# When the first layer's output weight is split: six of eight slices during the last gates instead of four

## The chip, the cores and the metric

The kernel runs on one core of a Trainium2 chip. Five engines work side by side, each through its own list of instructions in order: TensorE (PE in the profile; PEld is its weight load), VectorE (DVE), ScalarE (ACT), GpSimd (POOL) and SyncE (SP), which here mostly issues DMAs. The metric is the device time of one execution in microseconds, the median of several.

## The reference, cut to what matters

One inference step of two layers, a Mamba-2 SSD layer and a latent-attention (MLA) layer, over 1024 prompt tokens and 64 sample tokens (8 sequences of 8). The change touches the end of the SSD layer alone:

```
proj = einsum('btd,de->bte', h, w_in)          # z, x/B/C and dt
z = proj[..., :SSD_D_INNER]                    # the gate, 2048 columns
...
y, new_state = ssd_scan(xs, dt, a_head, bm, cm, ssm_state)
y = y + d_skip[:, None] * xs
y = y.reshape(b, t, SSD_D_INNER) * silu(z)
yg = y.reshape(b, t, SSD_GROUPS, SSD_D_INNER // SSD_GROUPS)       # 8 groups of 256
yg = yg * rsqrt(mean(yg * yg, axis=-1, keepdims=True) + NORM_EPS)
y = yg.reshape(b, t, SSD_D_INNER) * norm_w
out = einsum('bte,ed->btd', y, w_out)          # w_out: 2048 x 1024
h = h + out
```

All of it is in 32-bit floats. A product is made as three matmuls on split operands: a high part (a rounded copy, `fp32r`) and a low part (the difference), high x high, high x low and low x high.

## The kernel before, in words

**Tokens and groups.** The tokens are nine tiles: eight of 128 prompt tokens and one of 64 sample tokens. The SSD layer runs over eight groups of heads. A group has steps of its own (`Group.steps`, 21 yields): twelve for its four blocks of projection and convolution, then nine for its gates, one per token tile (`gates`, line 547; tile pz in PSUM, z in SBUF). While group g+1 takes its steps, group g is scanned (`ssd_scan`, with `ssd_chunks` for the chunks and `ssd_states` for the sample states).

**The gate of the last tile.** It has 64 rows, and its high and low parts are stacked on 128 partitions of one PSUM bank. `fold` (line 108) copies one half by ScalarE (line 109) and adds the other by VectorE (line 110); the addition sets the bank free. The projections, the gates (pz) and the output product (poa) share two such banks, tag "pj".

**The output product of the first half.** `w_out` has 16 slices of 128 rows. The first eight belong to groups 0 to 3, whose y is complete long before the end; their product (`pha`, tiles named ...a) is formed while the last group (7) is scanned, and that of the other eight (`phb`, ...b) after it. A slice is made ready in `wout_halves` (line 767): a load of 512 KB (line 770, SP's queue), the high part with the norm's weight by ScalarE (line 771) and the low part by VectorE (line 772). The first eight do not get buffers of their own: `wout_cols` writes them over the columns of the normed input, `k.xh` and `k.xl`, that belong to token tile kk, once the gates of that tile have been taken.

**When.** `last_steps` (line 782) wraps the steps of group 7. Steps 0 to 11 are blocks, step 12 + i is the gate of token tile i. After the steps in `WCOLS` it calls `wout_cols` for the next slice, with a load buffer out of the pool of the convolution's raw rows (tag "raw", two buffers; named wor in the profile). At the last of `WCOLS`, step 19, it also starts the output product's first part, `prep` of token tile 0. What is left of the eight slices is called for at line 953, after the pools of the projection are closed, with two load buffers of their own in the memory that those pools held (named wraw).

**The output product's steps.** `prep` (line 806) loads the y of one token tile (line 815), scales its groups (line 818), transposes it on TensorE (line 826) and splits it (tiles yha, yla). `ssd_out` (line 839) runs over the tiles: two halves of 512 columns, each a PSUM bank with three matmuls per slice (line 98 through `mm_tok`), then the addition to the residual (line 854, tile xra). `prep` of the next tile is called after the first half. The load of y has two pools, used in turn: tile 0, 2, 4 in one, 1, 3, 5 in the other, which is opened only with the late buffers.

**The order on the engines.** The program's text gives priorities; the order of the instructions on each engine and queue is fixed when the program is built, by a scheduler with a timeline of its own (`schedule_with_timeline_sim=True`). `issue_after(ins)` makes what is issued inside it stand behind `ins` on the same engine; it is an order, not a wait.

Of the kernel before, what the change touches and what calls it, by code (L numbers as in the profile page):

```python
# [11 lines left out]
ALU = mybir.AluOpType  # L12
# [43 lines left out]
NWA = 8  # L56
CA = 1
PAR = 0.62
WCOLS = (13, 15, 17, 19)
XDB = 2  # L60
WARM = (8, 2, 1)
SQ = (3, 3)
# [26 lines left out]
def mm_tok(nc, p, m, n, terms):  # L89
    ops = []  # L90
    for j, (a, b, a2, wh, wl) in enumerate(terms):
        if m == 64:
            x = [(p[:64, :n], a, wl), (p[:, :n], a2, wh)]
            ops += x if j else x[::-1]
        else:
            ops += [(p[:m, :n], *ab) for ab in ((a, wh), (a, wl), (b, wh))]
    for j, (o, a, b) in enumerate(ops):
        nc.tensor.matmul(o, a, b, start=(j == 0), stop=(j == len(ops) - 1))  # L98
        yield


def both(xh, xl, i, kk):
    t0, m = TILES[i]
    a = xh[:, kk, t0 : t0 + m]
    return (a, None, xh[:, kk, t0 : t0 + 128]) if m == 64 else (a, xl[:, kk, t0 : t0 + m], None)


def fold(nc, out, p, n):
    nc.scalar.copy(out[:64, :n], p[64:128, :n])
    nc.vector.tensor_tensor(out[:64, :n], out[:64, :n], p[:64, :n], op=ALU.add)  # L110


def open_pool(tc, name, bufs=1, space=None, **kw):
# [11 lines left out]
def split(k, hi, lo, src, eng=None, parts=0):  # L125
    nc = k.nc
    k.cast = nc.scalar.copy(hi, src)  # L127
    n = parts and hi.shape[1] // parts
    for a in range(parts):
        s = slice(a * n, a * n + n)  # L130
        (eng or nc.vector).tensor_tensor(lo[:, s], src[:, s], hi[:, s].bitcast(F32), op=ALU.subtract)
    if not parts:
        return (eng or nc.vector).tensor_tensor(lo, src, hi.bitcast(F32), op=ALU.subtract)  # L133
# [83 lines left out]
def rstd_of(k, out, ssq, n):  # L217
    nc = k.nc
    nc.vector.tensor_scalar(out, ssq, 1.0 / n, EPS, op0=ALU.mult, op1=ALU.add)
    m, n = out.shape[0], int(np.prod(out.shape[1:]))  # L220
    e = k.nhalf[:m, :n]
    if len(out.shape) == 3:
        e = e.rearrange("p (a b) -> p a b", a=out.shape[1])
    return nc.gpsimd.tensor_tensor(out, out, e, op=ALU.pow)
# [103 lines left out]
def load_parts(k, pool, src, nk, parts, tag, bufs, raws=None, rbufs=2, eng=None, late=None):  # L328
    n = nk // parts
    return [x for j in range(parts)  # L330
            for x in kslices(load_w(k, pool, src[128 * n * j : 128 * n * j + 128 * n], n, src.shape[1], tag, bufs,
                                    raws, rbufs, eng, late=late if j == parts - 1 else None), n)]
# [125 lines left out]
class Group:  # L458
# [88 lines left out]
    def gates(self):  # L547
        k, g, nc = self.k, self.g, self.k.nc
        w = k.I["ssd_w_in"][0]
        wz = k.wzd if g == 0 else load_parts(k, self.wp, w[:, 256 * g : 256 * g + 256], 8, 2 * WPARTS, "wi", WB, None, RB)  # L550
        self.z = []
        for i, (t0, m) in enumerate(TILES):
            if i % 5 == 0:
                z = self.gp.tile([128, 5, 256], F32, tag="z", name=f"z{g}{i}", bufs=3)
                self.z.append(z)
            n = 256 if g else 288
            p = self.psum.tile([128, 512], F32, tag="pj", name="pz", bufs=PB["pj"])
            drain(mm_tok(nc, p, m, n, [(*both(k.xh, k.xl, i, kk), *wz[kk])
                                       for kk in range(8)]))
            if g == 0:  # L560
                nc.vector.tensor_tensor(k.dtr[:m, i], p[:m, 256:288], k.dtb[:m], op=ALU.add)
                if m == 64:
                    nc.vector.tensor_tensor(k.dtr[:m, i], k.dtr[:m, i], p[64:128, 256:288], op=ALU.add)
            if m == 64:
                fold(nc, z[:, i % 5], p, 256)
            else:
                nc.scalar.copy(z[:m, i % 5], p[:m, :256])  # L567
            if i == 4:
                with k.tc.issue_after(k.yoc.ins) if g == G - 1 else nullcontext():
                    nc.scalar.activation(z, z, AF.Silu)  # L570
            yield
        nc.scalar.activation(z[:, :3], z[:, :3], AF.Silu)
        nc.scalar.activation(z[:64, 3], z[:64, 3], AF.Silu)
# [201 lines left out]
def wout_cols(k, kk, raw, ws):  # L775
    cs = slice(kk * 128, kk * 128 + 128)
    hi, lo = k.xh[:, :, cs], k.xl[:, :, cs]
    wout_halves(k, kk, raw, hi, lo)
    ws.append((hi, lo))


def last_steps(k, steps, rp, ws, out):
    for n, _ in enumerate(steps):
        if n in WCOLS:
            kk = len(ws)
            wout_cols(k, kk, rp.tile([128, RAW], F32, tag="raw", name=f"wor{kk}", bufs=2)[:, :D].rearrange(
                "p (k e) -> p k e", k=8), ws)
        if n == WCOLS[-1]:
            next(out)
        yield  # L790

# [9 lines left out]
class OutHalf:  # L801
# [4 lines left out]
    def prep(self, i, yp, psum):  # L806
        k, nc, tag, k0 = self.k, self.k.nc, self.tag, self.k0
        nk = NWA
        g0, ng = k0 // 2, nk // 2
        if self.rs is None:  # L810
            self.rs = k.cs.tile([128, 9, ng], F32, name="yrs" + tag)
            rstd_of(k, self.rs, k.yssq[:, :, g0 : g0 + ng], 256)
        t0, m = TILES[i]
        y = yp.tile([128, ng, 256], F32, tag="yt", name=f"yt{tag}{i}", bufs=1)
        nc.sync.dma_start(y[:m].rearrange("p g c -> p (g c)"),
                          k.y_d[t0 : t0 + m, k0 * 128 : (k0 + nk) * 128])
        for g in range(ng):
            nc.vector.tensor_scalar(y[:m, g], y[:m, g], self.rs[:m, i, g : g + 1], None, op0=ALU.mult)
        yh = yp.tile([128, nk, 128], F32R, tag="yh", name=f"yh{tag}{i}", bufs=1)
        yl = yp.tile([128, nk, 128], F32R, tag="yl", name=f"yl{tag}{i}", bufs=1)  # L820
        yv = y.rearrange("p g c -> p (g c)")
        for q in range(nk // 4):
            p = psum.tile([128, 512], F32, tag="tr", name=f"ytp{tag}{i}{q}", bufs=PB["tr"])
            for a in range(4):
                b = q * 4 + a
                nc.tensor.transpose(p[:, a * 128 : a * 128 + m], yv[:m, b * 128 : b * 128 + 128], k.ident[:m, :m])
            pv = p.rearrange("p (a t) -> p a t", a=4)[:, :, :m]
            qs = slice(q * 4, q * 4 + 4)
            split(k, yh[:, qs, :m], yh[:, qs, 64:] if m == 64 else yl[:, qs], pv)
            k.ycast = k.cast  # L830
        return yh, yl
# [40 lines left out]
def layer_ssd(k):  # L872
# [8 lines left out]
    with ExitStack() as st:  # L881
# [51 lines left out]
        for g in range(G - 1):  # L933
            nx = Group(k, g + 1, pools)
            steps = nx.steps() if g < G - 2 else last_steps(k, nx.steps(), rp, pha.ws, pa)
            done = 0
            w = 0
            for x in ssd_scan(k, gr, (sp, psum)):
                w += x
                while done < int(w + 0.01):  # L940
                    next(steps, None)
                    done += 1
            for _ in steps:
                pass
            gr = nx
# [50 lines left out]
def mla_in(k, right, mid):  # L996
    tc, nc, I = k.tc, k.nc, k.I
    k.g_d = k.dram.tile([8, 128, T], F32, name="g_d")
    with ExitStack() as st:
# [19 lines left out]
        with open_pool(tc, name="kg", bufs=1, side="right") as kg:  # L1019
            gk = gather_kpe(k, kg)  # L1020
            next(gk)
            page_rows(k, kg)
            for n in range(QG + 8):
                next(gates)
                if n >= QG:
                    next(gk)
            drain(gk)
# [7 lines left out]
        wkp = wk.enter_context(open_pool(tc, name="wpk", bufs=1, side="right"))  # L1035
        wkv = load_cw(k, wkp, rw, 512, 288, "ck")
        drain(gates)
        sg.close()
        wq = st.enter_context(open_pool(tc, name="wpc", bufs=1))
# [9 lines left out]
def mla_kv(k, sp, ws):  # L1049
# [8 lines left out]
    for i, (t0, m) in enumerate(TILES):  # L1058
        pk = k.psum.tile([128, 512], F32, tag="pj", name=f"pk{i}", bufs=PB["pj"])
        token_proj(k, pk, i, ws, 288)  # L1060
        if m == 64:
            pk, pk_ = sp.tile([128, 512], F32, tag="cqs", name="pk8", bufs=1), pk
            fold(nc, pk, pk_, 288)
# [392 lines left out]
def drain(g):  # L1456
    for _ in g:
        pass
# [621 lines left out]
```

## Time and profile before

| | us |
|---|---|
| median of 3 runs | 1930.48 |
| lowest and highest run | 1929.45, 1934.53 |
| profiled execution | 1939.72 |
| its span in the profile | 1937.9 |

The granted TensorE clock was 0.994 over the span. Times inside the program are microseconds from the start of the span. A name such as `poa<-xh,yha` is output and inputs of an instruction with the tiles' numbers left out. A bracket behind a row of the order of time tells how long the engine stood idle before it and which instruction on which engine ended that. Such a bracket is left out where the wait was very short.

### The profile page before, as it was taken

The page shows a single profiled execution, that of the slowest core. Times are in us where ns is not written, and L with a number is a line of the kernel's source. Part 1 is how long each engine was busy: PE and PEld are TensorE (multiplying, and loading weights), DVE is VectorE, ACT ScalarE, POOL GpSimd, SP SyncE. Part 2 cuts the span into 40 slices and gives each one's busy share as a digit, 9 for nine tenths or more (in the row PEclk, how much of TensorE's full clock was granted, in tenths as well). Part 3 has the DMA queues.
Part 4 walks back from the last instruction along what each step waited for, and adds up shares of the span by engine and source line. Part 5 has one row for each costly group of instructions (what it writes and reads, how often), then busy time and mean ns, then how long its engine had stood idle before and what let it go on. Part 6 is the DMA issues. An engine that isn't in the chain of part 4 may idle for free.

```text
span 1937.9 us, 33631 instructions
## 1 busy us (share of the span) xinstructions
PE 1894.9 (98%) x12023; PEld 1733.7 (89%) x12023; DVE 1209.1 (62%) x2500; ACT 1100.4 (57%) x2525; POOL 828.6 (43%) x1122
## 2 busy tenths in 40 slices
PE   9999999999999999899999999999999999899998
PEld 7999999999999999788788998998888888688887
DVE  5557676767676767755534114567877878766674
ACT  6467566666666766732214314436777777755552
POOL 2447555555655555443004222104333435854551
PEclk9999999999999999999999999999999999989999
DMA  5123323233333332644434342223111112645441
GB/s 166 50 78 90 94 80 100 82 106 87 93 89 92 89 93 88 202 145 172 168 109 127 114 163 86 72 96 92 48 47 43 53 42 82 212 142 155 156 128 39
DMA packets 181088, 202.02 MB, mean 104 GB/s; under 512 B 18829, under 2 KB 147609, under 8 KB 180537
## 3 DMA queue, kind: packets, MB, share of 16 engines
q1 hardware_dynamic: 175864, 180.08, 30.3%
q0 software_dynamic: 4976, 19.66, 3.0%
q8 instruction: 95, 1.56, 0.3%
q14 instruction: 73, 0.59, 0.1%
q10 hardware_dynamic: 80, 0.13, 0.0%
HBM read 146.52 MB, written 53.28 MB: 103 GB/s over the span
## 4 chain that ended last, share of the span: by engine, by line
PE 87%; DMA 4%; ACT 3%; DVE 3%; issue 1%; POOL 1%; SPq 0%; POOLq 0%; DVEq 0%; ACTq 0%
PE pj L86 24%; PE pz L98 7%; PE pq L98 6%; PE pob L98 5%; PE p L98 5%; PE poa L98 3%; PE py L638 3%; PE sc L86 3%; PE o L86 2%; PE sc L1376 2%; PE o L1439 2%; PE o L1441 2%; PE st L1408 2%; DMA M<-acs_d 2%; PE st L1409 2%; PE st L1410 2%
## 5 line engine op out<-in xcount | busy, mean ns | idle before, releaser
L86 PE MATMUL pj<-xl,wih 128*128 128x384 f32 (+1 forms) x768 | 255.4, 333 | 0.0
L86 PE MATMUL pj<-xh,wih 128*128 128x384 f32 (+1 forms) x768 | 252.9, 333 | 0.5 <-ACT raw L512 0.3
L86 PE MATMUL pj<-xh,wil 128*128 128x384 f32 (+1 forms) x768 | 252.9, 329 | 0.0
L1422 POOL TENSOR_TENSOR tl<-P,th 128x384 fp32r<-128x384 f32 (+1 forms) x96 | 90.6, 944 | 232.3 <-ACT P L1420 190.6
L526 DVE SCALAR_TENSOR_TENSOR acc<-raw,vec,acc 128x1112 f32<-128x1112 f32 x96 | 139.9, 1458 | 14.3 <-ACT acc L522 13.4
L98 PE MATMUL pz<-wih,xh 128*128 128x256 f32 x504 | 143.4, 288 | 2.5 <-ACT z L567 2.5
L86 PEld LDWEIGHTS pj<-xh,wih 128*128 128x128 f32 x768 | 143.8, 188 | 1.9 <-ACT xh L273 0.7
L86 PEld LDWEIGHTS pj<-xl,wih 128*128 128x128 f32 x768 | 144.5, 188 | 1.0
L86 PEld LDWEIGHTS pj<-xh,wil 128*128 128x128 f32 x768 | 144.4, 188 | 0.5
L98 PE MATMUL pz<-wil,xh 128*128 128x256 f32 (+1 forms) x504 | 139.6, 283 | 0.0
L1419 ACT ACTIVATE th<-st 128x512 fp32r<-128x512 f32 x192 | 94.6, 493 | 65.9 <-PE st L1415 50.3
L633 ACT ACTIVATE M<-M,tok 128x128 f32<-128x128 f32 (+1 forms) x288 | 91.0, 386 | 67.7 <-DVE M L629 67.2
L98 PE MATMUL pz<-wih,xl 128*128 128x256 f32 x448 | 128.9, 288 | 0.0
L1712 POOL TENSOR_TENSOR kvl<-pgr,kvh 128x256 fp32r<-128x256 f32 x128 | 96.5, 781 | 65.6 <-ACT kvh L1710 65.5
L133 DVE TENSOR_TENSOR wil<-wraw,wih 128x512 fp32r<-128x512 f32 x88 | 74.2, 849 | 40.7 <-ACT wih L127 34.0
L98 PEld LDWEIGHTS pz<-wih,xh 128*128 128x128 f32 x504 | 95.9, 190 | 3.5 <-ACT z L567 2.9
L1420 ACT ACTIVATE P<-st 128x512 f32<-128x512 f32 x192 | 93.5, 487 | 0.0
L98 PEld LDWEIGHTS pz<-wil,xh 128*128 128x128 f32 (+1 forms) x504 | 92.8, 184 | 0.3
L614 POOL TENSOR_TENSOR xdd<-xsT,tok 128x256 f32<-128x256 f32 x64 | 49.9, 779 | 90.2 <-ACT xsT L600 89.7
L98 PEld LDWEIGHTS pz<-wih,xl 128*128 128x128 f32 x448 | 85.3, 190 | 0.5
L1422 DVE TENSOR_TENSOR tl<-P,th 128x512 fp32r<-128x512 f32 x96 | 70.7, 737 | 19.5 <-ACT P L1420 19.3
L127 ACT CAST wih<-wraw 128x512 fp32r<-128x512 f32 x92 | 55.9, 616 | 43.9 <-PE pj L86 28.9
(834 smaller groups left out, 6295.1 us busy)
## 6 DMA issues: line engine op xcount, KB each, us to landing
wraw<-in_ssd_w_in SPq DMA_DIRECT2D x92, 256.0 KB
M<-acs_d SPq DMA_DIRECT2D x64, 256.0 KB
s<-in_state_ssm SPq DMA_DIRECT2D x32, 256.0 KB
y_d<-y SPq DMA_DIRECT2D x64, 128.0 KB
out_s_ssm<-s SPq DMA_DIRECT2D x32, 256.0 KB
wraw<-in_ssd_w_out SPq DMA_DIRECT2D x12, 512.0 KB
q_d<-qt SPq DMA_DIRECT2D x32, 192.0 KB
qp<-q_d SPq DMA_DIRECT2D x8, 768.0 KB
```

The costliest lines, as they stand in the source:

```text
L86: nc.tensor.matmul(out, a, b, start=(i == 0), stop=(i == n - 1))
L98: nc.tensor.matmul(o, a, b, start=(j == 0), stop=(j == len(ops) - 1))
L127: k.cast = nc.scalar.copy(hi, src)
L133: return (eng or nc.vector).tensor_tensor(lo, src, hi.bitcast(F32), op=ALU.subtract)
L526: last = nc.vector.scalar_tensor_tensor(acc, raw[:, j : j + n], k.convw[j][:, blk : blk + 1], acc, op0=ALU.mult, op1=ALU.add)
L614: nc.gpsimd.tensor_tensor(v3(xdd), v3(xsT), hb(2), op=ALU.mult)
L633: nc.scalar.activation(M[:m, h, :m], M[:m, h, :m], AF.Exp, bias=tk[:, 0, 4 * g + h : 4 * g + h + 1])
L638: nc.tensor.matmul(py[:m, h * 64 : h * 64 + 64], M[:m, h, :m], xsT[:m, h * 64 : h * 64 + 64], start=True, stop=True)
L1419: nc.scalar.activation(th[:, :n], ps[:, :n], AF.Exp, scale=SCALE)
L1420: nc.scalar.activation(P[:, :n], ps[:, :n], AF.Exp, scale=SCALE)
L1422: eng.tensor_tensor(tl[:, :n], P[:, :n], th[:, :n].bitcast(F32), op=ALU.subtract)
L1712: nc.gpsimd.tensor_tensor(rl[:, j], raw[:, j], rh[:, j].bitcast(F32), op=ALU.subtract)
```

## The change

Three edits. `WCOLS` gets six steps instead of four: after steps 13, 15, 17, 18, 19 and 20 instead of 13, 15, 17 and 19. Slices 0 to 2 keep their steps, slice 3 comes one step earlier, and slices 4 and 5 are called for after the gates of token tiles 7 and 8, with the two buffers of the raw rows. Slices 6 and 7 are left to line 953. The first `prep` stays at step 19, which is now written out. Third, `fold` returns its VectorE instruction, the gates of the last tile keep it as `k.zfold`, and `prep` of token tile 1 in the first half puts its scalings behind it on VectorE.

```diff
-WCOLS = (13, 15, 17, 19)
+WCOLS = (13, 15, 17, 18, 19, 20)
...
 def fold(nc, out, p, n):
     nc.scalar.copy(out[:64, :n], p[64:128, :n])
-    nc.vector.tensor_tensor(out[:64, :n], out[:64, :n], p[:64, :n], op=ALU.add)
+    return nc.vector.tensor_tensor(out[:64, :n], out[:64, :n], p[:64, :n], op=ALU.add)
...
             if m == 64:
-                fold(nc, z[:, i % 5], p, 256)
+                k.zfold = fold(nc, z[:, i % 5], p, 256)
...
-        if n == WCOLS[-1]:
+        if n == 19:
             next(out)
...
-        for g in range(ng):
-            nc.vector.tensor_scalar(y[:m, g], y[:m, g], self.rs[:m, i, g : g + 1], None, op0=ALU.mult)
+        with k.tc.issue_after(k.zfold.ins) if i == 1 and not k0 else nullcontext():
+            for g in range(ng):
+                nc.vector.tensor_scalar(y[:m, g], y[:m, g], self.rs[:m, i, g : g + 1], None, op0=ALU.mult)
```

## The prediction

> **What bounds the kernel now.** First the page: its span, the engines' share, and who carries the chain that ended last.
>
> ```profile
> span 1937.9 us, 33631 instructions
> PE 1894.9 (98%) x12023; PEld 1733.7 (89%) x12023; DVE 1209.1 (62%) x2500; ACT 1100.4 (57%) x2525; POOL 828.6 (43%) x1122
> PE 87%; DMA 4%; ACT 3%; DVE 3%; issue 1%; POOL 1%; SPq 0%; POOLq 0%; DVEq 0%; ACTq 0%
> ```
>
> TensorE is busy 98% of the span and holds 87% of the chain, so a change that moves no matmul out of the program can gain only where TensorE waits or runs slowly. Next I looked for that place around the edited lines. The output product of the first layer (tile poa, line 98) starts near 795 us; this is TensorE's order of time there (start, duration, engine, line, count; in brackets the idle time before and who ended it), the rows with a wait and two others:
>
> ```profile
> 800.56 0.47 PE L98 MATMUL poa<-xh,yha 128*128 128x512 f32 x1 [1.31 <-DVE z L110]
> ...
> 807.26 0.74 PE L98 MATMUL poa<-xh,yha 128*128 128x512 f32 x2 [1.47 <-ACT xh L771]
> ...
> 809.02 0.50 PE L98 MATMUL poa<-xl,yha 128*128 128x512 f32 x1 [0.62 <-DVE xl L772]
> ...
> 810.30 0.60 PE L826 MATMUL ytpa<-ident,yta 128*128 128x128 f32 x4
> ...
> 814.26 0.47 PE L595 MATMUL trp<-ident,acc 128*128 128x128 f32 x1 [2.04 <-DVE yla L133]
> ...
> 822.27 0.40 PE L98 MATMUL poa<-xh,yla 128*128 128x512 f32 x1
> ...
> 824.42 0.50 PE L98 MATMUL poa<-xh,yha 128*128 128x512 f32 x1 [0.76 <-DVE xra L854]
> ```
>
> These are the waits and the last matmul of tile 0 (822.27). Five waits, 1.31 + 1.47 + 0.62 + 2.04 + 0.76 = 6.20 us. Two (2.09 us) are for weight slices still being split on ScalarE (line 771, high part) and VectorE (line 772, low part); one is for the PSUM bank of the last gate, freed by line 110. Busy time by stretch, with granted clock (columns: PE, PEld, DVE, ACT, POOL, PEclk, DMA share, GB/s):
>
> ```profile
> 800.56:805.80 5.24, 5.23 (x25) 4.02 (x25) 4.12 (x7) 4.54 (x10) 2.04 (x1) 1.00 1.02 416
> 814.26:817.44 3.18, 3.18 (x12) 2.76 (x13) 2.63 (x4) 3.18 (x8) 0.46 (x1) 0.51 0.81 241
> 817.44:823.70 6.26, 6.12 (x42) 5.24 (x40) 5.84 (x13) 1.80 (x7) 5.38 (x8) 1.00 0.58 193
> 880.00:900.00 20.00, 20.00 (x114) 16.89 (x113) 9.95 (x19) 4.22 (x14) 5.46 (x8) 1.00 0.31 106
> ```
>
> After the 2.04 us wait TensorE runs 3.18 us at 0.51, losing 3.18 x 0.49 = 1.56 us. So all that this place holds is 6.20 + 1.56 = 7.8 us, 0.4% of the run. Later it is full again (20.00 of 20.00 at 880), so what is won before 824 should reach the end.
>
> **The change part by part.**
>
> *Two more slices in the gates.* Nothing is added to the sum of work: the loads, casts and subtractions of slices 4 and 5 move from after the gates to beside the last three. First what they cost and where they stand now (loads on SP's queue, casts on ScalarE, subtractions on VectorE; wor is the early buffer, wraw the late one):
>
> ```profile
> 776.86 0.33 SPq L770 DMA_DIRECT2D wor<-in_ssd_w_out  x1
> 796.36 0.90 SPq L770 DMA_DIRECT2D wraw<-in_ssd_w_out  x2
> 801.96 1.15 ACT L771 ACTIVATE xh<-wraw,vec 128x1024 fp32r<-128x1024 f32 x1 [0.67 <-DMA wraw<-in_ssd_w_out]
> 806.07 1.14 ACT L771 ACTIVATE xh<-wraw,vec 128x1024 fp32r<-128x1024 f32 x1
> 803.15 1.28 DVE L772 SCALAR_TENSOR_TENSOR xl<-wraw,vec,xh 128x1024 fp32r<-128x1024 f32 x1 [0.93 <-ACT xh L771]
> 807.26 1.71 DVE L772 SCALAR_TENSOR_TENSOR xl<-wraw,vec,xh 128x1024 fp32r<-128x1024 f32 x1
> 816.23 1.28 DVE L772 SCALAR_TENSOR_TENSOR xl<-wraw,vec,xh 128x1024 fp32r<-128x1024 f32 x1
> 819.79 1.63 DVE L772 SCALAR_TENSOR_TENSOR xl<-wraw,vec,xh 128x1024 fp32r<-128x1024 f32 x1
> ```
>
> A slice costs ScalarE 1.15 us and VectorE 1.28 to 1.71 us. Where they go:
>
> ```profile
> 780.90 1.64 DVE L772 SCALAR_TENSOR_TENSOR xl<-wor,vec,xh 128x1024 fp32r<-128x1024 f32 x1
> 782.66 1.43 DVE L772 SCALAR_TENSOR_TENSOR xl<-wor,vec,xh 128x1024 fp32r<-128x1024 f32 x1
> 790.07 0.42 DVE L656 TENSOR_TENSOR y<-py,tok 128x256 f32<-128x256 f32 x1 [3.43 <-PE py L86]
> 785.51 0.37 ACT L567 COPY z<-pz 128x256 f32<-128x256 f32 x1
> 788.37 0.38 ACT L669 COPY fo<-pf 128x256 f32<-128x256 f32 x1 [1.78 <-PE pf L667]
> 791.25 0.37 ACT L567 COPY z<-pz 128x256 f32<-128x256 f32 x1 [0.99 <-PE pz L98]
> 789.08 0.61 POOL L624 TENSOR_TENSOR xD<-xsT,dsk 64x256 f32<-64x256 f32 x1 [4.39 <-ACT xsT L600]
> ```
>
> The early buffers are two, so slices 4 and 5 can load only when the subtractions of 2 and 3 end, at 782.5 and 784.1. The late loads took 801.96 - 796.36 = 5.6 us on busy queues; an estimate from the third early load, issued at 774.24 by the row below, whose cast began at 778.94, is 4.7 us.
>
> ```profile
> 774.24 0.33 SPq L770 DMA_DIRECT2D wor<-in_ssd_w_out  x1
> 778.94 1.15 ACT L771 ACTIVATE xh<-wor,vec 128x1024 fp32r<-128x1024 f32 x1
> ```
>
> So the data stands at 787.2 to 788.1 and 788.8 to 789.7. ScalarE has holes of 1.78 us before 788.37 and 0.99 us before 791.25, VectorE one of 3.43 us before 790.07: the work of 2.3 and 2.6 to 3.4 us fits, with little to spare. I take its cost there as nothing; between nothing and the whole 2.3 us of casts in front of the gates' copies lies the range. Their queue is SP's, and behind them on it stand these two:
>
> ```profile
> 783.54 0.38 SPq L712 DMA_DIRECT2D s<-in_state_ssm  x1
> ...
> 794.48 1.83 SPq L628 DMA_DIRECT2D M<-acs_d  x1
> ```
>
> The state load could go out 0.6 us later (behind 784.1), for transposes that run after 800; the scan's next M load comes ten microseconds on. Neither is late.
>
> [...]
>
> What it buys: the product of tile 0 is two halves over eight slices, three matmuls each. The chain of waits gives their pace:
>
> ```profile
> 824.42 5.29 PE poa L98 x22
> ```
>
> That is 0.24 us each, so the slices 4 and 5 of both halves are 12 x 0.24 = 2.9 us of TensorE work that no longer has to wait. Six go right after the first half's twelve, ahead of 800.56, and cover the 1.31 us in which TensorE waited for line 110. The stretch 800.56 to 805.80 holds 18 of these matmuls then as now. Slices 6 and 7 take the late buffers, and so the loads of 796.36 and the places of 801.96 and 806.07; slice 6's six matmuls (1.4 us) fill the 1.47 us before 807.26. Slice 7 is where 5 was: the 0.62 us stays. Tile 0 is complete near 810 instead of 822.5, and TensorE has 1.31 + 1.47 = **2.8 us** less idle time. Its sums can be taken from the banks about ten microseconds sooner, so the **0.76 us** before 824.42 goes too. What is late next is tile 1's transposed input (line 133, yla), which ended the 2.04 us: it hangs on scaling, transposes and casts that do not change places, so I leave this wait and the half clock after it.
>
> *The hold.* It puts tile 1's scaling behind line 110 on VectorE. Which scaling is tile 1's?
>
> ```profile
> 791.33 0.87 PE ytpa L826 x8
> ```
>
> ```profile
> 792.24 0.33 SPq L815 DMA_DIRECT2D yta<-y_d  x1
> 797.78 0.66 SPq L815 DMA_DIRECT2D yta<-y_d  x1
> 798.12 1.97 DVE L818 TENSOR_SCALAR yta<-yta,yrsa 128x256 f32<-128x256 f32 x4 [1.35 <-DMA yta<-y_d]
> 800.02 0.40 DVE L110 TENSOR_TENSOR z<-z,pz 64x256 f32<-64x256 f32 x1
> 808.89 1.61 DVE L818 TENSOR_SCALAR yta<-yta,yrsa 128x256 f32<-128x256 f32 x4
> ```
>
> Tiles alternate between two buffers. The first row is the first tile's transposes, ending at 792.20; the load of 792.24 goes out that moment, so it refills the first buffer: it is tile 2's. Tile 1's is that of 797.78, scaled at 808.89, already behind 800.02. What stands before line 110 is tile 2's scaling, which is not held. In the present order the hold changes nothing; it acts only if the new order would put tile 1 first. I count it at 0, with bounds of 1.31 us gained (if line 110 moved up and nothing else hid it) and 1.6 us lost (the four scalings, if VectorE then has nothing else ready). Behind it on VectorE wait the transposes of tile 1.
>
> *Sum:* 2.8 + 0.76 = 3.5 us. The profiled execution took 1939.72 us, 9.2 us over the median of 1930.48; the same saving on the median gives **1927.0 us** (-0.18%).
>
> **The rivals.**
>
> *The 2.04 us wait goes as well.* VectorE loses two subtractions (2.9 us) between 814 and 823, ScalarE two casts, and matmuls of tile 1 could run where TensorE now waits. Then all 2.04 and the 1.56 us of slow clock come on top: 3.5 + 3.6 = 7.1, with the 0.62 us 7.8 us, or 1923 us. For it: VectorE is 5.84 of 6.26 us busy there. Against: yla is split before those subtractions.
> [...]
>
> *Nothing is won.* The late slice that ends last still gates tile 0, or the order puts slices 6 and 7 where they stood (816.23 and 819.79 on VectorE). Then tile 1 starts at 824 as now: 1930.5 us, or 1929 with the 1.31 us covered.
>
> *A wait in the gates takes its place.* ScalarE is in order. If the casts of slices 4 and 5 are put ahead of the gates' copies (785.51 and its neighbours), those stand until the loads land: 788.8 - 785.5 = 3.3 us each, the two gate banks fill, TensorE stops and restarts at half clock (1.6 us each, from the 814.26 row). Twice 4.9 is 9.8 us lost against 3.5 won: 1937 us. It decides at a load that lands later than the copy behind it is due. Against: ScalarE's holes are near the landing.
>
> **How the numbers follow.** Forecast 0.49 (own range 1925 to 1929); all waits gone 0.28; nothing won 0.12; a wait in the gates 0.11. 0.3%, about what a measurement of this kernel can tell from no change, is 5.8 us. All waits gone passes it nearly always: faster 0.27. Slower, only the last rival: 0.11. Same: 0.62. The range: down to 1923 less 2 us, the runs before spreading over 5 us; up to no gain plus the upper half of that spread: 1921 to 1933.
>
> **What would show it.** Six casts from the early buffer and two from the late one; two more loads near 783 and 785; tile 0's banks emptied near 811; no wait before the first matmul of its second half nor before 807; a span near 1934.4 us. A half clock still near 814 is my case; none, the faster rival. TensorE idle between 785 and 792 is the slower rival. Wrong it would be if the builder's scheduler, which lays out each engine's order anew, moved work elsewhere.

## The result, and the profile after

| | before | after |
|---|---|---|
| median, us (22 runs each) | 1931.33 | 1925.90 |
| lowest and highest run, us | 1929.19, 1937.85 | 1921.63, 1932.08 |
| profiled execution, us | 1939.72 | 1923.23 |
| ratio after : before | | 0.9968, 95% interval [0.9961, 0.9976] |

By the ratio the change saves 0.32% of 1931.33 us, about 6.2 us (4.6 to 7.5); the two medians differ by 5.4. The forecast was a time of 1927.0 us from a saving of 3.5: the sign is right, the time is near and inside the stated range, and the saving is short by almost half. That the time comes nearer than the saving is partly luck: the forecast started from 1930.48 us, the median of three runs, which is 0.85 under that of the 22. The 0.3% that the prediction's chances turn on lies inside the interval.

The page of the changed kernel: span, shares, and the chain that ended last.

```profile
span 1921.4 us, 33638 instructions
PE 1886.8 (98%) x12023; PEld 1727.7 (90%) x12023; DVE 1205.7 (63%) x2500; ACT 1099.4 (57%) x2525; POOL 827.6 (43%) x1122
PE 85%; ACT 4%; DVE 4%; DMA 3%; issue 1%; POOL 1%; SPq 0%; POOLq 0%; DVEq 0%; ACTq 0%
```

Nothing here says where the time went, and the two spans differ by 16.5 us, far more than the runs do. The place is told by two groups of instructions: the first matmuls of tile poa (the first half's product) and of tile pob (the second half's). The columns are shortest, median and longest duration in ns, then first and last start. The first two rows are of before, the last two of the changed kernel.

```profile
L98 PE MATMUL poa<-xh,yha x144: 387/390/796, 794.7 to 933.7; 128*128 128x512 f32 x144
L98 PE MATMUL pob<-woh,yhb x144: 389/393/498, 935.2 to 1038.1; 128*128 128x512 f32 x144
```

```profile
L98 PE MATMUL poa<-xh,yha x144: 387/393/503, 793.9 to 923.4; 128*128 128x512 f32 x144
L98 PE MATMUL pob<-woh,yhb x144: 389/393/497, 924.9 to 1028.2; 128*128 128x512 f32 x144
```

From first poa to first pob is "the stage" below: 935.2 - 794.7 = 140.5 us before, 924.9 - 793.9 = 131.0 after. It starts at 793.9, and at 794.4 and 794.9 in two more executions of the same order (e1 and e12 below), for 794.7 and 794.3 before: the two slices in the gates cost nothing that can be seen. From the first pob to the end of the span it is 1937.9 - 935.2 = 1002.7 and 1921.4 - 924.9 = 996.5 us. In the other profiled runs this rest goes from 996.4 to 1003.2. It does not go with the edit: two executions of one order can lie at both ends (after and e12 below, 996.5 and 1001.1). It goes with the clock late in the run: between 1660 and 1720 us the granted clock is 0.91 to 0.94 on the mean in the ten executions whose rest is under 1000 us (0.94 in the changed kernel's), and 0.86 to 0.89 in the four whose rest is over it (before is one of these, with 0.86). This is why the stage and the ratios are compared below, and not spans.

What TensorE waited for in the changed kernel from 785 to 940 us (sum, number, longest):

```profile
PE poa L98 <- ACT yha L127: 1.9, 1, 1.9
PE pob L98 <- DVE xra L857: 0.3, 2, 0.2
PE ytpb L827 <- DVE ylb L133: 0.3, 1, 0.3
```

The waits on late slices, on line 110 and on tile 0's residual sum (line 854 of before) are gone. The one on the second token tile's transposed input is there as before, 1.94 us for 2.04:

```profile
811.11 0.50 PE L98 MATMUL poa<-xh,yha 128*128 128x512 f32 x1 [1.94 <-ACT yha L127]
```

No half clock follows it in this execution. Stretches of 30 us (length, then PE, PEld, DVE, ACT, POOL busy, clock, DMA share, GB/s), of before and then of the changed kernel; the sums run to 910 us, and the rows that are not shown are full:

```profile
790.00:820.00 30.00, 24.18 (x146) 19.95 (x146) 23.55 (x44) 22.53 (x52) 10.70 (x14) 0.94 0.68 230
820.00:850.00 30.00, 29.14 (x163) 24.70 (x162) 16.74 (x32) 8.38 (x25) 13.99 (x23) 1.00 0.49 165
850.00:880.00 30.00, 29.00 (x163) 24.05 (x162) 19.07 (x43) 12.67 (x40) 14.71 (x21) 1.00 0.44 133
sum 120.00, PE 112.31 PEld 93.55 DVE 74.36 ACT 49.78 POOL 46.90; mean PE 28.08 PEld 23.39 DVE 18.59 ACT 12.45 POOL 11.73
```

```profile
790.00:820.00 30.00, 28.06 (x166) 23.34 (x165) 22.61 (x47) 20.31 (x49) 13.21 (x19) 1.00 0.75 252
820.00:850.00 30.00, 30.00 (x183) 25.92 (x181) 20.79 (x41) 11.19 (x33) 16.69 (x26) 1.00 0.47 151
sum 120.00, PE 118.06 PEld 99.57 DVE 76.24 ACT 50.44 POOL 52.21; mean PE 29.51 PEld 24.89 DVE 19.06 ACT 12.61 POOL 13.05
```

TensorE stood idle 120 - 112.31 = 7.69 us of these 120 us before and 1.94 after, and that is more than the waits up to 824: a full microsecond was idle between 850 and 880, where the prediction had looked at 880 to 900 only and found it full. The rows of before:

```profile
860.46 0.47 PE L731 MATMUL sn<-bb,x 96*128 96x512 f32 x1 [0.32 <-DVE S L652]
...
863.90 0.31 PE L724 MATMUL pv<-sl,cblk 128*32 128x128 f32 x2 [0.68 <-DVE sl L133]
```

Where the slices went: the casts of slices 4 and 5 by ScalarE began at 785.20 and 787.86, with 1.26 us of waiting for the second load, and TensorE waited for nothing there. The casts of the two late slices began at 798.39 and 799.84; the first two of the four late ones before began at 801.96 and 806.07. On VectorE the order is new:

```profile
795.73 0.41 DVE L110 TENSOR_TENSOR z<-z,pz 64x256 f32<-64x256 f32 x1
796.06 1.49 DVE L819 TENSOR_SCALAR yta<-yta,yrsa 128x256 f32<-128x256 f32 x4
...
805.29 1.61 DVE L819 TENSOR_SCALAR yta<-yta,yrsa 128x256 f32<-128x256 f32 x4
```

Line 110 now stands ahead of the scaling at 796.06. That is tile 2's, which is not held; tile 1's, which is, comes at 805.29. SP's queue also sends the late loads about 4 us sooner, at 792.23 for 796.36. So three things differ: two slices, line 110, late loads. Which of them counts is the first question of the experiments.

### The profile page after: what moved, and what is told of

It reads as the page before. It is cut to its first block, busy times and chain, and to the rows that moved or that the text cites. A ratio compares the mean times of both kernels' runs of the same rounds, so it can differ in the third digit from the quotient of the medians.

```text
span 1921.4 us, 33638 instructions
## 1 busy us (share of the span) xinstructions
PE 1886.8 (98%) x12023; PEld 1727.7 (90%) x12023; DVE 1205.7 (63%) x2500; ACT 1099.4 (57%) x2525; POOL 827.6 (43%) x1122
## 4 chain that ended last, share of the span: by engine, by line
PE 85%; ACT 4%; DVE 4%; DMA 3%; issue 1%; POOL 1%; SPq 0%; POOLq 0%; DVEq 0%; ACTq 0%
PE pj L86 22%; PE pz L98 8%; PE pq L98 6%; PE p L98 5%; PE pob L98 5%; PE poa L98 4%; PE py L638 3%; PE sc L86 2%; PE o L86 2%; PE sc L1377 2%; PE o L1440 2%; PE o L1442 2%; PE st L1409 2%; PE st L1410 2%; PE st L1411 2%; PE o L1441 2%
## 5 line engine op out<-in xcount | busy, mean ns | idle before, releaser
L98 PE MATMUL pz<-wil,xh 128*128 128x256 f32 (+1 forms) x504 | 139.6, 283 | 0.0
```

## The experiments

The theory: the slices are the cause. TensorE's waits near 800 are one shortage of ready work, and only more ready matmuls end them. The rivals: the order that came along (line 110, the late loads, tile 1's input), and the half clock. Each kernel ran beside kernel before on the same chip; the chips differ from group to group, so the ratios are compared.

| | slices in the gates | ratio to before, 95% interval | stage, us | half clock, us |
|---|---|---|---|---|
| before | 4 | 1 | 140.5 | 3.4 |
| e2 hold alone | 4 | 1.0011 [1.0, 1.0023] | 138.7 | 6.8 |
| e8 line 110 first | 4 | 1.0016 [1.0003, 1.003] | 140.3 | 6.8 |
| e6 tile 1's y early | 4 | 0.9997 [0.9984, 1.001] | 138.6 | 3.4 |
| e11 four, filled | 4 | 1.0012 [0.9998, 1.0027] | 141.0 | 3.4 |
| e3 five | 5 | 0.9993 [0.9982, 1.0004] | 136.8 | 6.8 |
| after | 6 | 0.9968 [0.9961, 0.9976] | 131.0 | none |
| e1 six, no hold | 6 | 0.9956 [0.994, 0.9973] | 131.1 | none |
| e12 after again | 6 | 0.9969 [0.9956, 0.9982] | 132.8 | 3.4 |
| e5 tile 1's y early | 6 | 0.9973 [0.996, 0.9986] | 134.2 | 3.4 |
| e9 cast first | 6 | 0.9971 [0.9958, 0.9983] | 132.0 | none |
| e4 seven | 7 | 0.9961 [0.9945, 0.9976] | 130.6 | none |
| e7 seven, y early | 7 | 0.9963 [0.995, 0.9976] | 130.3 | none |
| e10 seven, cast first | 7 | 0.9958 [0.9946, 0.9971] | 130.6 | none |

The stage is the difference of the two first starts as above. The last column is how long the granted clock stood at 0.50 near 800 to 825 us. The orders of after, e1 and e12 are the same, and so are those of before and e2.

**e1: six slices without the hold.**

```diff
-        with k.tc.issue_after(k.zfold.ins) if i == 1 and not k0 else nullcontext():
+        with nullcontext():
```

> Six slices, no hold of tile 1's scaling. Theory (the slices do it all, the hold changes no order): as the changed kernel, 1925 to 1927 us and ratio near 0.997 to before, stage from the first matmul of poa to the first of pob 131.0 us as in the changed kernel (131.0), the low parts' addition of line 110 at once behind line 634 on VectorE. Rival (the hold brings the bank free earlier): 1.3 us or more of wait comes back before the second half of tile 0, stage 132.3 or more.

Ratio 0.9956, stage 131.1. The order of the instructions is that of the changed kernel on all five engines. The hold does nothing here.

**e2: the hold alone.**

```diff
-WCOLS = (13, 15, 17, 18, 19, 20)
+WCOLS = (13, 15, 17, 19)
```

> Four slices as before, with the hold. Theory (slices): as before, ratio 1.000, stage 140.5 us, line 110 still behind a scaling, which is tile 2's, with 1.31 us of TensorE wait. Rival (the hold): line 110 moves ahead, 1.31 us gone, stage 139 or less. The stage length also tells how far a profiled stage repeats.

Ratio 1.0011 [1.0, 1.0023], and every engine's order is that of before. So e2 is a second execution of before: its stage, 138.7 against 140.5, says how far one order repeats (1.8 us).

**e3: five slices.**

```diff
-WCOLS = (13, 15, 17, 18, 19, 20)
+WCOLS = (13, 15, 17, 19, 20)
```

> Five slices in the gates (after steps 13, 15, 17, 19, 20), three late. Theory (each slice that is early takes six matmuls, 1.4 us, out of the late pile, and its cast and subtraction off ScalarE and VectorE): stage between, 134 to 137 us, 1928 to 1929 us. Rival (a threshold: the gain comes when line 110 stands ahead of tile 2's scaling and the late loads ahead of the scan's M load, whatever the number of slices): stage 131 to 132.5 as with six.

Ratio 0.9993, stage 136.8. Line 110 stands first and the late loads go out at 793.16, as after the change, and yet hardly anything is won, less than the theory's 1928 to 1929 us asked for. One long wait took the place of the five (TensorE):

```profile
814.05 0.45 PE L595 MATMUL trp<-ident,acc 128*128 128x128 f32 x1 [4.46 <-DVE yla L133]
```

The gain isn't in proportion to the slices, and it doesn't come with the new order alone.

**e4: seven slices.**

```diff
-WCOLS = (13, 15, 17, 18, 19, 20)
+WCOLS = (13, 15, 16, 17, 18, 19, 20)
```

> Seven slices in the gates (after steps 13, 15, 16, 17, 18, 19, 20), one late. Theory (after the change the slices no longer bound; tile 1's transposed input ends the last wait, 1.94 us): stage 130.5 to 131.5, time as the changed kernel within 1 us. Rival (the late slices still cost): stage 129.5 or less, 1924 us. Other side: casts in the gates hold the gates' copies, TensorE waits before the first poa matmul and the run is slower than with six by 1 to 3 us.

Ratio 0.9961, stage 130.6. A slice's cast (ScalarE) waits for its load, the cast of tile 0's input (yha) stands behind it, and TensorE waits for that. This is the mechanism of the prediction's slower rival, in small (first TensorE, then ScalarE):

```profile
796.38 0.50 PE L98 MATMUL poa<-xh,yha 128*128 128x512 f32 x1 [1.17 <-ACT yha L127]
793.78 1.15 ACT L771 ACTIVATE xh<-wor,vec 128x1024 fp32r<-128x1024 f32 x1 [2.06 <-DMA wor<-in_ssd_w_out]
```

It costs 1.17 us. The stage starts 2.5 us later than after the change, at 796.4 for 793.9, but 2.0 of that have another source: the same scan product starts at 702.56 us here and at 700.54 there, before any slice is asked for. In this execution the clock is halved from 13.84 to 17.25 us, and after the change it is not (1.00 over the same stretch).

**e5: six slices, tile 1's y loaded early.** The changed kernel's one wait was for tile 1's transposed input; the load was put ahead of the late slices'.

```diff
+        k.y1 = ys[1].tile([128, 4, 256], F32, tag="yt", name="yta1", bufs=1)
+        nc.sync.dma_start(k.y1.rearrange("p g c -> p (g c)"), k.y_d[128:256, :1024])
...
-        y = yp.tile([128, ng, 256], F32, tag="yt", name=f"yt{tag}{i}", bufs=1)
+        y = k.y1 if i == 1 and not k0 else yp.tile([128, ng, 256], F32, tag="yt", name=f"yt{tag}{i}", bufs=1)
```

`prep` skips its own load for this tile.

> Six slices as in the changed kernel; the load of token tile 1's y goes out ahead of the late slices' loads instead of behind them, so its scaling stands ahead of the late subtractions. Theory A (what is left of the wait before the second token tile, 1.94 us in the changed kernel, is tile 1's transposed input, late because its y is loaded and scaled last): that wait falls under 0.5 us, the stage from the first matmul of the first half's product to the first of the second half's takes about 129 us (131.0 less 1.94), the time about 1924 us. Rival B (ScalarE sets it: the exponentials that stand ahead of the cast yha there): the wait stays between 1 and 2 us, the stage near 131, the time as the changed kernel's.

Theory A falls. Rival B has the right engine and the right time (ratio 0.9973), but not the sizes: the wait grows to 2.83 us, and the stage to 134.2, with a half clock of 3.4 us in it. Tile 1 is scaled at 802.02 instead of 805.29. The order of time on ScalarE in e5 shows what stands before the cast of its transposed input:

```profile
809.68 0.42 ACT L662 ACTIVATE xD<-y 128x256 f32<-128x256 f32 x1 [1.97 <-DVE y L661]
...
811.49 2.44 ACT L633 ACTIVATE M<-M,tok 128x128 f32<-128x128 f32 x8
813.84 0.56 ACT L127 CAST yha<-ytpa 128x512 fp32r<-128x512 f32 x1
```

Eight exponentials stand ahead of the cast, and behind a squaring that waits 1.97 us for VectorE.

**e6: the same load early, with four slices.** The edit of e5 with the `WCOLS` of e2.

> Four slices as before, with tile 1's y loaded early alone. Theory A (the half clock near 814 follows from the one wait of 2.04 us for tile 1's input): wait and half clock both go, the three earlier waits (1.31, 1.47, 0.62) stay; the stage takes about 138.7 - 2.0 - 1.6 = 135 us, the time about 1928. Rival C (the clock is halved because TensorE has too little to do over several microseconds while slices are missing, whatever waits there are): the half clock stays somewhere between 805 and 820, the stage is 137 us or more, the time within 2 us of before.

Ratio 0.9997, stage 138.6: nothing, as the rival has it. TensorE's waits in e6:

```profile
PE poa L98 <- DVE xl L772: 3.0, 3, 1.9
PE trp L595 <- DVE yla L133: 0.9, 2, 0.5
PE poa L98 <- ACT xh L771: 0.7, 1, 0.7
PE poa L98 <- DVE z L110: 0.7, 1, 0.7
```

The 2.04 us wait is down to 0.9, and the wait on the slices' low parts is up to 3.0. The half clock is there, 7 us later, at 820.87 (0.94 on the mean from 820 to 850, 1.00 from 790 to 820).

**e7: seven slices, the last two after step 20, tile 1's y early.** To the edit of e5:

```diff
-WCOLS = (13, 15, 17, 18, 19, 20)
+WCOLS = (13, 15, 17, 18, 19, 20, 20)
...
-        if n in WCOLS:
+        for _ in range(WCOLS.count(n)):
```

> Seven slices, the seventh asked for after the last gate together with the sixth, and tile 1's y early. If the casts are kept out of the way of the gates' copies, the stage takes 129 us or less and the time is 1923 to 1925; if the seventh slice's cast stands ahead of the gates' last copies as with seven slices before (there 1.2 us before the first product and a start 2 us later), the gain is given back in the gates: stage short, time as the changed kernel's, 1925 to 1927.

Ratio 0.9963, stage 130.3 from 794.9: the later place spares most of e4's wait before the first product (0.34 us for 1.17), and the time is the changed kernel's within the intervals.

**e8: four slices, line 110 first.** With e2's `WCOLS`; the hold is put on the tile whose scaling stood before line 110.

```diff
-        with k.tc.issue_after(k.zfold.ins) if i == 1 and not k0 else nullcontext():
+        with k.tc.issue_after(k.zfold.ins) if i == 2 and not k0 else nullcontext():
```

> Four slices as before; the hold is put on token tile 2's scaling instead of tile 1's, so that the addition that sets the last gate's bank free stands ahead of it on VectorE. Theory A (the gain comes from the two more slices, which give TensorE something to do): the 1.31 us wait goes or moves to the next late slice, the other waits and the half clock stay, the stage takes 137 to 139 us, the time is within 1.5 us of before. Rival D (the gain comes from the order that the change brought along: the addition ahead of the scaling): the stage falls to 131 to 134 us and the time to 1926 to 1928.

Ratio 1.0016 [1.0003, 1.003], stage 140.3. Line 110 no longer ends any wait, and the waits on late slices are longer than before's 1.47 and 0.62 (TensorE's waits in e8):

```profile
PE poa L98 <- ACT xh L771: 1.9, 2, 1.6
PE poa L98 <- DVE xl L772: 1.6, 3, 0.6
```

Here too 1.31 us won is lost again behind it. The hold also made the scheduler lay out all five engines a little differently, so this is one new order with four slices, and not the old one with line 110 moved.

**e9: six slices, tile 1's cast ahead of the exponentials.** What e5 pointed to.

```diff
-        with k.tc.issue_after(k.ycast.ins) if g == G - 1 and i == 0 else nullcontext():
+        with k.tc.issue_after((k.ycast1 if i else k.ycast).ins) if g == G - 1 and i < 3 else nullcontext():
...
-            k.ycast = k.cast
+            k.ycast, k.ycast1 = k.cast, k.ycast if i == 1 and q else k.cast
```

> Six slices as in the changed kernel; the exponentials of chunks 1 and 2 are held on ScalarE behind the first cast (yha) of token tile 1. Theory (the wait of 1.94 us that is left in the changed kernel is this cast, standing on ScalarE behind 2.45 us of exponentials that wait for their own load): the wait falls to 0.5 us or less, the stage takes 129 to 130 us, the time is 1 to 2 us under that of the changed kernel beside it. Rival (the exponentials are due as soon, so their delay of 0.6 us and more comes back as a wait for the chunk's products): the stage stays at 131, the time the same.

The 1.94 us wait is gone, and the time is 1928.62 us beside 1928.71 of the changed kernel (e12): the rival. In its place (TensorE's waits in e9):

```profile
PE trp L595 <- DVE yla L133: 1.0, 1, 1.0
PE poa L98 <- DVE xra L855: 1.0, 2, 0.7
PE cb L626 <- DVE yo L727: 0.6, 1, 0.6
```

**e10: seven slices and the cast first.** The edits of e9 and of e7's `WCOLS`.

> Seven slices, the sixth and seventh both asked for after the last gate, and the same hold of the exponentials behind tile 1's first cast. If the waits that are left all hang on this cast, the stage takes 129 us or less and the time is 2 us under that of the changed kernel beside it; if not, the time is the changed kernel's within 1 us.

Ratio 0.9958 [0.9946, 0.9971] beside 0.9969 [0.9956, 0.9982] for e12: 2.35 us less by the medians, which the intervals don't separate. Its waits from 785 to 940 add up to 1.1 us (TensorE's waits in e10):

```profile
PE poa L98 <- ACT yha L127: 0.7, 1, 0.7
PE py L638 <- DVE M L634: 0.2, 1, 0.2
PE pob L98 <- ACT yhb L127: 0.2, 1, 0.2
```

Yet the stage is 130.6, only 0.4 us under the changed kernel's, with 2.0 us less idle time in it. The two stages do not hold the same work (the whole stage, of the changed kernel and then of e10; columns as above):

```profile
793.89:924.91 131.02, 128.66 (x714) 106.75 (x713) 82.11 (x165) 53.98 (x140) 49.40 (x64) 1.00 0.57 191
793.60:924.23 130.63, 130.25 (x726) 107.90 (x726) 82.20 (x172) 55.07 (x142) 49.78 (x66) 1.00 0.59 193
```

That of e10 has twelve more matmuls: eight of the scan (tile py, 101 for 93), which run ahead of the first poa product after the change, and four transposes of the second half's input (tile ytpb, 16 for 12). The eight are in the stages of e4 and e7 too, and those of e3, e8 and e9 have four transposes less. So between these orders the stage compares to about a microsecond only; those of before and after hold 714 each.

**e11: four slices, TensorE kept busy.** With e2's `WCOLS`; sixteen products that nothing reads.

```diff
+            [nc.tensor.matmul(p[:, :256], k.xh[:, 0, :128], k.xh[:, 0, :256], start=True, stop=True) for _ in range(8 if i == 1 and not k0 else 0)]
             for a in range(4):
```

> Four slices with the hold (the order of before), and sixteen more products of 128x256 whose results are overwritten at once, eight in front of each bank of token tile 1's transposes: about 16 x 0.12 = 1.9 us of TensorE work where it is idle before. Theory (the clock is halved because TensorE works too little over some microseconds; 3.2 to 7.5 us at half clock are part of what the four slices cost): no half clock between 800 and 825 or half as much of it, and the stage is 1 to 3 us shorter than the 138.7 of the four slices although more is computed. Rival (the half clock is of no account, or comes from something else): the half clock stays, or it goes and the stage stays at 138 to 141 us.

Ratio 1.0012, stage 141.0, and the clock is halved for 3.4 us, as in before. On all five engines some other instructions changed places as well. The run is inconclusive on the clock's price: the products wait for their own bank (1.15 us in front of the first eight), and the wait for tile 1's input behind them is 2.23 us, so the stretch in which TensorE was to be kept busy was not filled.

**e12: the changed kernel again.**

> The changed kernel once more, beside the three others: a time 5 to 7 us under the kernel before, a stage of 131 us with one wait of 1.9 us, and no half clock.

Ratio 0.9969, with the same single wait, 1.94 us; but here the half clock comes, and the stage is 132.8. Three executions of one order (after, e1, e12) show it once, and this tells the price of one half clock of 3.41 us: the stage is 1.6 to 1.8 us longer.

## Why the prediction was right or wrong

**The 1.31 + 1.47 us that slices 4 and 5 fill: right.** Both waits are gone and the first half runs through. That it is the slices is shown by all orders together: the six with six or seven slices gain (ratios 0.9956 to 0.9973), and the five with four or five do not (0.9993 to 1.0016), though line 110 stands first in e3 and e8 and the late loads go out early in e3. No run has six slices with line 110 in its old place, and why the fifth slice brings so much less than the sixth is not shown, beyond e3's wait of 4.46 us. **The 0.76 us on line 854: right**, it is gone. **No cost in the gates: right**; e4 shows the rival's mechanism at one slice more, with 1.17 us. The subtractions of slices 4 and 5 took 1.28 us each, the least of the 1.28 to 1.71 of before. GpSimd's product at 789.61, beside the second of them (789.04), took 1.19 us, for 0.61 at 789.08 before; why is not shown.

**The hold counted as 0: right**, and for the reason given. The scaling ahead of line 110 was tile 2's. e1 and e2 show the hold moves no instruction. The bound "1.31 us gained (if line 110 moved up and nothing else hid it)" was too high: in e8 line 110 moved up and the wait came back at the next slice.

**The 2.04 us that "I leave": right in size**, 1.94, but the reason given is only part of it. The prediction had it hang on scaling, transposes and casts that do not change places. Of these it is the cast, and the cast is late by its place on ScalarE, behind exponentials, in before (first two rows) as after the change:

```profile
811.73 1.28 ACT L633 ACTIVATE M<-M,tok 128x128 f32<-128x128 f32 x4 [3.35 <-DVE M L629]
812.92 0.56 ACT L127 CAST yha<-ytpa 128x512 fp32r<-128x512 f32 x1
```

```profile
808.13 2.45 ACT L633 ACTIVATE M<-M,tok 128x128 f32<-128x128 f32 x8 [0.86 <-DVE M L629]
810.49 0.56 ACT L127 CAST yha<-ytpa 128x512 fp32r<-128x512 f32 x1
```

e5 brought the scaling forward by 3 us and the wait grew. And the wait isn't a reserve by itself: e9 took it away and got nothing.

**The step that failed is the sum, "2.8 + 0.76 = 3.5 us": a term too small, and one missing.** The idle time fell by 7.69 - 1.94 = 5.75 us against the profile of before. e2 is the same order as before; its sum over the same stretches:

```profile
sum 120.00, PE 114.59 PEld 95.14 DVE 73.72 ACT 50.49 POOL 46.33; mean PE 28.65 PEld 23.78 DVE 18.43 ACT 12.62 POOL 11.58
```

That is 5.41 us idle, 3.47 more than after. So idle time gives 3.5 to 5.75 us. What the forecast left out of it: "the 0.62 us stays" (it went: the late loads leave 4 us sooner, and no late slice is waited for), and the 1.0 us between 860 and 864, from "later it is full again", which was read off one stretch that began too late. Why that microsecond goes is not shown.

The missing term is the clock. "I leave this wait and the half clock after it" tied the half clock to one wait of 2.04 us. e2 has a half clock of 6.8 us without any wait over 1.42 us, and two of three executions of the changed order have none behind a wait of 1.94. In the two executions of the order of before it stands for 3.4 and 6.8 us, a mean of 5.1; in the three of the changed order for 3.4, none and none, 1.1. By an estimate from the granted clock of 0.50, a microsecond at half clock costs at most half, and after, e1 and e12 bear the size out (3.41 us at half clock, 1.6 to 1.8 us of stage): at most (5.1 - 1.1) / 2 = 2.0 us. With the idle time of the two executions of before, (5.75 + 3.47) / 2 = 4.6, that makes up to 6.6, against 6.2 measured.

The agreement is no proof. The shares are means of two and three traced executions, and the stages of the same executions differ by more, 139.6 - 131.6 = 8.0 us on the mean. The whole stage of before, beside that of the changed kernel shown with e10:

```profile
794.74:935.21 140.47, 132.31 (x714) 108.18 (x713) 86.95 (x167) 56.20 (x143) 51.50 (x64) 0.99 0.56 185
```

TensorE is busy 3.65 us longer there with the same 714 matmuls, and the half clock of 3.41 us explains at most 1.7 of it, by the same estimate. The cause of the rest, about 2 us, stays open. By the same reckoning e2, with 133.26 us busy and 6.83 at half clock, leaves 1.2.

**The faster rival**, all waits and the half clock gone at 1923 us, missed as well: the wait stayed. "A half clock still near 814 is my case; none, the faster rival" can't be read at all, since one order shows both.

## What to carry to other kernels

A group of short waits around one place is often one shortage, and removing one wait hands its time to the next: e6, e8 and e9 each took away one to two microseconds of the wait they aimed at and won nothing, while more ready work (two slices) ended four waits at once. When a change alters the order of an engine, sum TensorE's idle time to the end of the stage, not up to the last wait that the change names, and count the matmuls in the two stages before comparing their lengths. And don't read a half clock as the price of the wait in front of it: e2 has 6.8 us of it without any wait over 1.42 us, and after and e1 have none behind a wait of 1.94.

## What the runs showed of the hardware

**How long the half clock stood.** In the eight executions that have one near 800 to 825 us, the granted clock stood at 0.50 for 3.4 us (before, e5, e6, e11 and e12) or for 6.8 (e2, e3 and e8). In e2 (columns as above), the stretch in front of it and two in it:

```profile
803.90:807.30 3.40, 1.49 (x5) 0.97 (x6) 2.21 (x6) 3.39 (x11) 0.72 (x1) 0.99 1.00 387
807.30:810.70 3.40, 2.88 (x8) 1.78 (x8) 3.40 (x6) 0.82 (x3) 1.42 (x2) 0.50 0.66 225
810.70:814.10 3.40, 3.14 (x18) 2.50 (x17) 2.78 (x6) 2.34 (x7) 0.00 (x0) 0.51 0.49 165
```

**What TensorE did in front of it.** In e2 it was busy 1.49 us of these 3.40, in pieces, with no idle time over 1.42 us. In e12 it was busy 1.46 of 3.40 us:

```profile
809.10:812.50 3.40, 1.46 (x14) 1.04 (x11) 2.81 (x5) 3.38 (x11) 0.00 (x0) 0.99 0.11 39
812.50:815.90 3.40, 3.40 (x11) 2.60 (x10) 2.02 (x5) 2.42 (x8) 0.85 (x2) 0.51 0.96 274
```

In after, whose order is that of e12, a stretch is as thin, and the clock stays at 1.00 in it and behind it, to 820 us (the rows of 30 us with the result):

```profile
808.60:812.00 3.40, 1.46 (x9) 0.72 (x7) 2.90 (x6) 3.40 (x12) 0.00 (x0) 1.00 0.10 37
```

So neither the busy time of such a stretch nor the wait in it, 1.94 us in both, tells in these two whether a half clock follows. Why one execution of an order has it and another has none is not shown; no run set it.
